# Two gate chunks beside the end of the attention, two more ahead of the first branch product, in a two-layer trunk on one Trainium2 core

## The chip, the cores and the metric

The kernel runs on one core of one Trainium2 chip. The metric is the device time of one execution, in microseconds; the median of three runs before the change is 2620.59 us (2617.87 to 2622.11). The profile comes from one further execution, which took 2614.91 us.

## What is computed

One inference step of a trunk of two layers over 128 context and 512 latent tokens (640 columns in all), width 1024, in fp32. Each layer normalizes and modulates its input, runs four token mixers on one input projection, merges them by gates, and adds a feed-forward part. Of the reference, what matters here:

```
def mixer(xn, lp, ctx, rope_cs):
    z = xn @ lp['w_in']
    ...
    y_attn = attention(q, k, v).reshape(b, l, MLA_HEADS * V_DIM)
    y_ssm, ssm_final = s5_branch(u_ssm, h0, ..., lp['w_glu'])
    y_fft = fourier_branch(u_fft)
    y_conv = g_b * short_conv(g_c * h_in, lp['conv_w'])
    branches = jnp.stack([y_ssm, y_fft, y_attn.astype(y_ssm.dtype), y_conv], axis=2)
    proj = jnp.einsum('blkw,kwd->blkd', branches, lp['w_branch'])
    gates = jax.nn.sigmoid(xn @ lp['w_gate'] + lp['b_gate']).reshape(b, l, N_BRANCH, D_MODEL)
    out = jnp.sum(gates * proj, axis=2) @ lp['w_out']
    return out, ckv_n, k_pe, ssm_final

def layer(x, cond, lp, ctx, rope_cs):
    sh_m, sc_m, g_m, sh_f, sc_f, g_f = modulation(cond, lp['w_ada'], lp['b_ada'])
    xn = rms_norm(x, lp['norm_mix_g']) * (1 + sc_m) + sh_m
    mix, ckv_n, k_pe, ssm_final = mixer(xn, lp, ctx, rope_cs)
    x = x + g_m * mix
```

## The kernel before

Tokens lie in the free dimension (two halves of 320 columns, one PSUM bank each), channels on the partitions. Each fp32 product is made of three matmuls of reduced type: high half times high half, low half of the weights, low half of the data. The halves are made on the way: a cast on ScalarE gives the high one (`whi`, `xh`, `yb`), a subtraction on VectorE the low one (`wlo`, `xl`, again `yb`, whose buffer first receives the raw tile).

`mixer_in` runs the attention (a generator whose steps are put between other work), four chunks of the short convolution, and then waits until the attention's generator is through. `mixer_out` then opens a pool and starts three things: the **merges**, the **SSM** (four blocks, `ssm_block`, as a side generator) and the **modulations** (a side generator).

- `merges` goes through 32 pairs of a gate and a branch product, in the order of branches 1, 3, 2, 0 with 8 output chunks d each. A gate is one chunk of 8 k steps of 6 matmuls (48 of 128x320), a sigmoid on ScalarE into a tile `m_s`. A branch product is 4 k steps (24 matmuls) on the tiles `yb` of the branch; VectorE multiplies it with the gate's tile into `acc` (L1434, or L1436 and L1437). Each gate stands one pair ahead of its product. The product's weights serve two values of d. The four `yb` tiles of the next branch are loaded by GpSimd's DMA queue (L1401), two before the last product of a branch and two behind it, and split (L320, L321). Chunks rotate through two PSUM tiles called `main`.
- An SSM block loads its factors, does two groups of 8 matmuls into `side` tiles, 16 copies to `s_t` on ScalarE (L1303 to L1306), multiplies and two scans on VectorE (L1315 to L1329), more multiplies, then 24 matmuls and an activation `s_y`. The decay tile `s_dec` has one buffer; GpSimd copies into it (L1280).
- `modulations` brings 32 pieces of 512 KB through one buffer (`ada`, L693), and VectorE makes two products with a running sum of each (L696), so that a load waits for the products of the piece before. Behind each eighth piece a bias is added (L698). The gate of the residual is among these sections.

The order on each engine is made ahead of the run by a scheduler from the order in which the program emits its work. Side generators are emitted by a planner's clock: it adds for each matmul about 0.136 us, and a generator comes on when the clock has passed its due time. The first modulation piece comes 12 us after the start, one each 10.5 us after that; the first SSM block 12 us after the start. By that clock a gate is about 6.5 us and a branch product about 3.3. What isn't done by the end of the merges is emitted there.

Behind the merges the output product runs (chunks of 48 matmuls on the `xh`, `xl` tiles, same two `main` tiles), and VectorE adds each chunk to the residual (`x`, L1457), which frees its banks for the chunk after next.

The lines that matter most: the gate ahead of its product, the SSM's start, and the constants

```
            if n + 1 < len(order):
                k2, d2 = order[n + 1]
                ...
                gate(k2, d2)
...
            def blocks():
                yield 12.0
...
MOD_START = (12.0, 90.0)
MOD_PACE = (10.5, 12.0)
```

Of the kernel before, what the change touches and what calls it, by code (L numbers as in the profile page):

```python
# [11 lines left out]
AF = mybir.ActivationFunctionType  # L12
# [7 lines left out]
KD = 8  # L20
LAT = 512
CTX = 128
NT = LAT + CTX
HALF = NT // 2
# [15 lines left out]
SSM_LOAD, SSM_STEP, SSM_LAST = 12.0, 3.0, 6.0  # L40
P_DELAY, PV_DELAY = 5.0, 1.8
TABLES_PACE = 1.5
ROT_START, ROT_PACE = 8.0, 6.0
MOD_START = (12.0, 90.0)
MOD_PACE = (10.5, 12.0)

V_GMIX, V_GFFN, V_BADA, V_BGATE, V_QA, V_KVA, V_GQ, V_GK, V_CONV, V_DSK, NV = (
    0, 8, 16, 64, 96, 99, 101, 102, 103, 115, 123)
# [157 lines left out]
class Program:  # L206
# [1175 lines left out]
        return out  # L1382


    def merges(self, pool, l, ycm, acc, xs, ssm):

        nc = self.nc
        two = lambda ap: ap.rearrange("p (a b) -> p a b", a=2)
        yb = lambda: self.t(pool, [128, NT], "yb", F32R, bufs=12)
        order = [(k, d) for k in (1, 3, 2, 0) for d in range(KD)]  # L1390
        ys = {k: [] for k in range(4)}
        sig, w, out = [], None, []

        def load(k, tiles):
            for i in tiles:
                hi, lo = yb(), yb()
                if k == 0:
                    self.split(hi, lo, ycm[i].rearrange("p t k -> p (t k)"))
                else:
                    y = lo.bitcast(F32)  # L1400
                    nc.gpsimd.dma_start(out=y, in_=self.d_br[l][{1: 1, 2: 0, 3: 2}[k]][i])  # L1401
                    self.split(hi, lo, y)
                ys[k].append((hi, lo))

        def gate(k, d):
            n = k * KD + d
            pg = self.chunk(self.A["wgate"][l, n], KD, xs)
            s = self.t(pool, [128, NT], "m_s")
            nc.scalar.activation(out=two(s), in_=pg[:, :, :HALF], func=AF.Sigmoid,
                                 bias=self.vec[l][:, V_BGATE + n:V_BGATE + n + 1])  # L1410
            sig.append(s)

        load(1, range(4))
        gate(*order[0])
        for n, (k, d) in enumerate(order):
            if k == 0 and d == 0:
                ys[0] = self.glu(pool, l, ycm, ys[0])
            if n + 1 < len(order):
                k2, d2 = order[n + 1]
                if d2 == 0:  # L1420
                    if k2 == 0:
                        self.need(ssm)
                    load(k2, range(2))
                gate(k2, d2)
            else:
                for i in range(KD - 1):
                    self.merged(l, acc, out, i)
            s = sig.pop(0)
            if d % 2 == 0:
                w = self.weights(self.A["wbr"][l, k, d // 2].rearrange("p a k m -> p (a k m)"), 1024)  # L1430
            pp = self.main_ps()
            self.gemm(pp, w, 512 * (d % 2), 128, 128, ys[k], range(4))
            if n < KD:
                self.anchor = nc.vector.tensor_mul(out=two(acc[d]), in0=pp[:, :, :HALF], in1=two(s))  # L1434
            else:
                self.anchor = nc.vector.tensor_mul(out=two(s), in0=pp[:, :, :HALF], in1=two(s))  # L1436
                nc.vector.tensor_add(out=acc[d], in0=acc[d], in1=s)  # L1437
            if d == KD - 1 and n + 1 < len(order):
                load(k2, range(2, 4))
        self.merged(l, acc, out, KD - 1)  # L1440
        return out

# [18 lines left out]
    def start(self, pool, x, norm, tags, tables):  # L1461
# [76 lines left out]
    def mixer_in(self, l, xs, first, tables):  # L1538

        nc, tc = self.nc, self.tc  # L1540
        A = self.A
        with tc.tile_pool(name=f"p1a{l}", bufs=8, reuse_waits="tile") as pa:
            with tc.tile_pool(name=f"p1f{l}", bufs=4, reuse_waits="tile") as pf:
                def consts(*names):
                    for name in names:
                        t = self.t(pa, {"cs": [128, 256], "ksel": [128, 64], "tk": [128, 6, 64], "selq": [128, 2, 32],
                                        "tq": [128, NT]}[name], name, bufs=1)
                        nc.sync.dma_start(out=t, in_=A[name])
                        setattr(self, name, t)
                if l > 0:  # L1550
                    self.tables = self.side(self.ssm_tables(tables, l, TABLES_PACE))
                lat = self.latents(pa, pf, l, xs, first, consts)
                for i in range(4):
                    self.ssm_input(pf, l, i, self.chunk(A["win"][l, 5 + i], KD, xs))
                consts("cs", "selq", "tq")
                dft = self.t(pf, [128, 2, 2, 257], "dft", bufs=1)
                nc.scalar.dma_start(out=dft, in_=A["dft"])
                dftc = self.t(pf, [128, 2, 128], "dftc", bufs=1)
                nc.scalar.dma_start(out=dftc, in_=A["dftc"])
                ff = []  # L1560
                for i in range(4):
                    ps = self.chunk(A["win"][l, 9 + i], KD, xs)
                    if i > 1:
                        self.need(ff[i - 2])
                    u = self.t(pf, [128, NT], "ct")
                    nc.scalar.copy(out=u.rearrange("p (a b) -> p a b", a=2), in_=ps[:, :, :HALF])
                    ff.append(self.side(self.fourier(pf, l, i, u, dft, dftc, ff[-1] if ff else None), True))
                self.need(*ff)
            with tc.tile_pool(name=f"p1k{l}", bufs=1, reuse_waits="tile") as pk:
                self.need(*lat)  # L1570
                self.keys_values(pk, pa, l)
                norms = self.queries(pk, pa, l)
                self.need(self.tables)
                tables.release()
                with tc.tile_pool(name=f"p1c{l}", bufs=3, reuse_waits="tile") as pc:
                    att = self.attention(pa, pc, l, norms)
                    self.rots = self.side(self.rotations(
                        l, lambda: self.t(pc, [128, 1024], "rotations", bufs=2), ROT_PACE, ROT_START))
                    for i in range(4):
                        self.conv(pc, l, i, xs)  # L1580
                    self.need(*att)
                    self.need(self.rots)

    def ssm_input(self, pool, l, i, ps):
        nc = self.nc
# [8 lines left out]
    def mixer_out(self, l, xs):  # L1594

        tc = self.tc
        with tc.tile_pool(name=f"p2{l}", bufs=2, reuse_waits="tile") as p:
            acc = [self.t(p, [128, NT], "acc", bufs=KD) for _ in range(KD)]
            ycm = [self.t(p, [128, 8, 80], "ycm", bufs=4) for _ in range(4)]

            def blocks():
                yield 12.0
                for b in range(4):
                    yield from self.ssm_block(p, l, b, ycm[b])
            ssm = self.side(blocks())
            self.modulations(p, l, range(2, 6), MOD_START[0], MOD_PACE[0], 1)
            ms = self.merges(p, l, ycm, acc, xs, ssm)
            self.need(self.modside)
            return ms

    def tail(self, l, ms):
# [107 lines left out]
    def emit(self):  # L1719
        with ExitStack() as ctx:  # L1720
            self.setup(ctx)
            ctx.enter_context(self.tc.manual_schedule(engines={mybir.EngineType.PE}))
            nc, tc = self.nc, self.tc
            tables = tc.alloc_tile_pool(name="p0t", bufs=2, side="right", reuse_waits="tile")
            with tc.tile_pool(name="p0", bufs=8, reuse_waits="tile") as p:
# [10 lines left out]
                xs, first = self.start(p, x, norm, tags, tables)  # L1736
            for l in range(L):
                if l == 0:
                    for k in range(KD):
                        self.tap(f"xh{l}_{k}", xs[k][0].bitcast(F32))  # L1740
                if l > 0:
                    tables = tc.alloc_tile_pool(name=f"p0t{l}", bufs=2, side="right", reuse_waits="tile")
                self.mixer_in(l, xs, first, tables)
                ms = self.mixer_out(l, xs)
                r = self.tail(l, ms)
                if r is not None:
                    xs, first = r
# [17 lines left out]
```

## Time and profile before

| what | value |
|---|---|
| median of 3 runs | 2620.59 us (2617.87 to 2622.11) |
| profiled execution | 2614.91 us, of which the span is 2613.1 |
| mean granted TensorE clock | 0.985 |
| instructions | 44975 |
| TensorE, VectorE, ScalarE, GpSimd busy | 97%, 69%, 40%, 7% of the span |
| HBM | 119 GB/s over the span |

The span is the time from the first to the last profiled instruction; 1.8 us of the execution lie around it. Layer 0 takes about the first half, layer 1 the second. In a timeline a row is a run of like instructions: start, duration, engine, line, operation, output and input tiles (buffer numbers left out), a count, and in brackets the idle time of the engine before it and what ended it. Neighbours on an engine overlap in part, so that the distance of two starts is shorter than a duration.

### The profile page before, as it was taken

What the parts mean: (1) busy time and instruction counts of PE and PEld (TensorE: products, weight loads), DVE (VectorE), ACT (ScalarE), POOL (GpSimd) and SP (SyncE); (2) the same over time, 40 slices, a digit from 0 to 9 for tenths busy, and PEclk for the clock granted to TensorE, in tenths of its full rate; (3) what the DMA queues carried; (4) which work ended last, traced back from release to release, by engine and by line L of the source; (5) the groups of instructions that cost most, each with busy time, mean ns of one, the idle gap of its engine ahead of it and who ended that gap; (6) DMA issues with size and microseconds to landing.
All of it is one profiled execution on the core that took longest, in us unless ns stands there. A gap on an engine that the chain in (4) does not pass through costs nothing.

```text
span 2613.1 us, 44975 instructions
## 1 busy us (share of the span) xinstructions
PE 2537.7 (97%) x18038; PEld 2434.7 (93%) x18038; DVE 1801.4 (69%) x3581; ACT 1054.0 (40%) x1793; POOL 188.6 (7%) x316
## 2 busy tenths in 40 slices
PE   7999999999999999999999999999999998999999
PEld 5988898999999899999979888989999998999999
DVE  5889764776555787876669897657676548666755
ACT  5335544333223543433453344443332226433433
POOL 0110000111000100000021100011200001000000
PEclk8999999999999999999999999999999999999999
DMA  6452115565444133433235322156644331222222
GB/s 254 130 157 96 54 61 175 166 210 172 129 122 155 51 104 119 122 97 88 79 115 151 123 98 74 46 185 207 197 158 125 118 113 57 82 82 89 79 79 86
DMA packets 121201, 313.85 MB, mean 120 GB/s; under 512 B 35616, under 2 KB 46432, under 8 KB 120608
## 3 DMA queue, kind: packets, MB, share of 16 engines
q1 hardware_dynamic: 101680, 250.52, 30.9%
q0 software_dynamic: 16432, 55.39, 6.2%
q10 hardware_dynamic: 2880, 5.06, 0.5%
q8 instruction: 142, 2.33, 0.4%
q14 instruction: 67, 0.55, 0.1%
HBM read 268.12 MB, written 42.80 MB: 119 GB/s over the span
## 4 chain that ended last, share of the span: by engine, by line
PE 82%; issue 10%; DVE 5%; ACT 3%; POOL 0%; DMA 0%; ACTq 0%; DVEq 0%; POOLq 0%
PE main L239 72%; PE side L239 8%; PE side L243 1%; DVE wlo L321 1%; DVE xl L543 1%; ACT xh L541 0%; ACT whi L320 0%; DVE tl L321 0%; ACT pq L1027 0%; DVE hh L569 0%; DMA yb<-d_br 0%; POOL d_r L1260 0%; DVE hh L538 0%; ACT P L924 0%; DVE hl L538 0%
## 5 line engine op out<-in xcount | busy, mean ns | idle before, releaser
L239 PE MATMUL main<-xh,whi 128*128 128x320 f32 x2848 | 740.0, 317 | 8.2 <-ACT xh L541 5.4
L239 PE MATMUL main<-xl,whi 128*128 128x320 f32 x2848 | 724.7, 312 | 6.7 <-DVE xl L321 4.5
L239 PE MATMUL main<-xh,wlo 128*128 128x320 f32 x2848 | 722.4, 311 | 0.0
L320 ACT CAST whi<-wraw 128x1024 fp32r<-128x1024 f32 (+2 forms) x318 | 297.6, 936 | 773.0 <-PE main L239 610.5
L239 PEld LDWEIGHTS main<-xh,whi 128*128 128x128 f32 x2848 | 494.7, 190 | 32.3 <-issue 19.3
L239 PEld LDWEIGHTS main<-xl,whi 128*128 128x128 f32 x2848 | 498.8, 190 | 11.5 <-DVE xl L321 5.7
L239 PEld LDWEIGHTS main<-xh,wlo 128*128 128x128 f32 x2848 | 499.2, 190 | 0.0
L321 DVE TENSOR_TENSOR wlo<-wraw,whi 128x1024 fp32r<-128x1024 f32 (+2 forms) x318 | 344.9, 1085 | 217.6 <-ACT whi L320 214.6
L239 PE MATMUL main<-yb,whi 128*128 128x320 f32 x1152 | 231.2, 312 | 4.4 <-ACT yb L320 4.4
L1457 DVE SCALAR_TENSOR_TENSOR x<-main,ada,x 128x320 f32<-128x320 f32 (+2 forms) x240 | 94.0, 434 | 193.2 <-PE main L239 193.0
L696 DVE SCALAR_TENSOR_TENSOR ada_j<-ada,ada_c 128x1024 bf16<-128x1024 f32 x160 | 194.8, 1217 | 3.8 <-DMA ada<-wada 3.2
L239 PEld LDWEIGHTS main<-yb,whi 128*128 128x128 f32 x1152 | 184.3, 189 | 5.3 <-ACT yb L320 4.9
L239 PE MATMUL main<-hh,whi 128*128 128x320 f32 x704 | 165.0, 310 | 1.0 <-ACT hh L320 1.0
L239 PE MATMUL main<-hl,whi 128*128 128x320 f32 x704 | 164.5, 309 | 0.0
L239 PE MATMUL main<-hh,wlo 128*128 128x320 f32 x704 | 164.3, 309 | 0.0
L239 PE MATMUL main<-th,whi 128*128 128x320 f32 x480 | 149.2, 311 | 0.0
L239 PE MATMUL main<-th,wlo 128*128 128x320 f32 x480 | 149.1, 311 | 0.0
L239 PE MATMUL main<-tl,whi 128*128 128x320 f32 x480 | 149.0, 310 | 0.0
L321 DVE TENSOR_TENSOR wlo<-wsum,whi 128x512 fp32r<-128x512 f32 (+1 forms) x120 | 103.6, 864 | 51.9 <-ACT whi L320 50.6
L320 ACT CAST whi<-wsum 128x512 fp32r<-128x512 f32 (+1 forms) x120 | 91.6, 763 | 114.9 <-PE main L239 110.5
L239 PE MATMUL main<-yb,wlo 128*128 128x320 f32 x576 | 132.0, 311 | 0.0
L239 PEld LDWEIGHTS main<-hh,whi 128*128 128x128 f32 x704 | 118.6, 188 | 4.1 <-issue 2.6
(346 smaller groups left out, 3766.6 us busy)
## 6 DMA issues: line engine op xcount, KB each, us to landing
ada<-wada SPq DMA_DIRECT2D x96, 512.0 KB, 4.2
wraw<-wfi SPq DMA_DIRECT2D x88, 512.0 KB, 3.5
wraw<-wgate SPq DMA_DIRECT2D x64, 512.0 KB, 3.6
wraw<-win SPq DMA_DIRECT2D x50, 512.0 KB, 3.6
wraw<-wfo SPq DMA_DIRECT2D x48, 384.0 KB, 3.2
wraw<-wbr SPq DMA_DIRECT2D x32, 512.0 KB, 3.6
d_f<-t_G POOLq DMA_DIRECT2D x16, 512.0 KB, 4.7
d_et<-t_et POOLq DMA_DIRECT2D x16, 512.0 KB, 4.6
```

Of the source, the lines that this page charges most:

```text
L239: self.nc.tensor.matmul(out, lhsT, rhs, **kw)
L243: self.nc.tensor.transpose(out, in_, ident)
L320: self.nc.scalar.copy(out=hi, in_=src)
L321: self.nc.vector.tensor_sub(out=lo, in0=src, in1=hi.bitcast(F32))
L543: nc.vector.scalar_tensor_tensor(out=xl[:, a:b], in0=t[:, a:b], scalar=B[:, s:s + 1], in1=xh.bitcast(F32)[:, a:b], op0=ALU.add, op1=ALU.su ...
L696: nc.vector.scalar_tensor_tensor(out=junk, in0=w, scalar=1.0, in1=sc[:, s, :], op0=ALU.mult, op1=ALU.mult, accum_out=self.ada[l][:, o + t, ...
L1457: self.anchor = nc.vector.scalar_tensor_tensor(out=x[:, o:o + n], in0=p, scalar=gcol[:, s:s + 1], in1=x[:, o:o + n], op0=ALU.mult, op1=ALU ...
```

## The change

The list of pairs goes to module level. A method `gate` makes one gate chunk and its sigmoid. `mixer_in` emits the first two gates behind the convolution chunks and ahead of the point where the attention has to be through, with the sigmoids in tiles of the convolution's pool, which stays open and is handed on. `merges` begins with these two, emits two more gates ahead of the first branch product, and then none until the third; from there each gate stands one pair ahead, as before. Behind the second product the convolution's pool is closed, a pool for the SSM's tiles is opened, and the SSM is started, without the 12 us of delay. The first two tiles of the next branch are loaded ahead of the gate instead of behind it. The modulations' start and pace are the same.

```diff
+MERGES = [(k, d) for k in (1, 3, 2, 0) for d in range(KD)]
...
+    def gate(self, l, n, xs, s):
+        pg = self.chunk(self.A["wgate"][l, n], KD, xs)
+        self.nc.scalar.activation(out=s.rearrange("p (a b) -> p a b", a=2), in_=pg[:, :, :HALF], func=AF.Sigmoid,
+                                  bias=self.vec[l][:, V_BGATE + n:V_BGATE + n + 1])
+        return s
...
         load(1, range(4))
-        gate(*order[0])
+        done = len(sig)
         for n, (k, d) in enumerate(order):
             if k == 0 and d == 0:
                 ys[0] = self.glu(pool, l, ycm, ys[0])
-            if n + 1 < len(order):
-                k2, d2 = order[n + 1]
-                if d2 == 0:
-                    if k2 == 0:
-                        self.need(ssm)
-                    load(k2, range(2))
-                gate(k2, d2)
-            else:
+            if d == KD - 1 and n + 1 < len(order):
+                if order[n + 1][0] == 0:
+                    self.need(ssm)
+                load(order[n + 1][0], range(2))
+
+            while done < min(n + 2 if n else 4, len(order)):
+                kg, dg = order[done]
+                sig.append(self.gate(l, kg * KD + dg, xs, self.t(pool, [128, NT], "m_s")))
+                done += 1
+            if n + 1 == len(order):
...
+            if n == 1:
+                ssm = start_ssm()
...
+                sig = [self.gate(l, MERGES[n][0] * KD + MERGES[n][1], xs, self.t(pc, [128, NT], "ct"))
+                       for n in range(2)]
+                self.need(*att)
+                self.need(self.rots)
+        return pc, sig
...
+            pc, sig = early
+            pools = []
+
             def blocks():
-                yield 12.0
                 for b in range(4):
-                    yield from self.ssm_block(p, l, b, ycm[b])
-            ssm = self.side(blocks())
+                    yield from self.ssm_block(pools[0], l, b, ycm[b])
+
+            def start_ssm():
+                pc.release()
+                pools.append(tc.alloc_tile_pool(name=f"p2s{l}", bufs=2, side="right", reuse_waits="tile"))
+                return self.side(blocks())
```

How this moves instructions, at three places. Lines of the changed file are one higher from the list on.

TensorE at the end of the attention in layer 0, before: scores (`side<-ak,at`), transposes of softmax rows (`side<-ident,P`), products with v (`side<-PT,v`), and the first gate (`main<-xh,whi`).

```order
L239 MATMUL side_728_4642<-ak_4288,at_4236 128x128
L243 MATMUL side_731_4653<-ident,P_4625 128x128
L243 MATMUL side_733_4657<-ident,P_4649 128x128
L239 MATMUL side_733_4657<-PT_4655,v_2140 64x128
L239 MATMUL side_733_4657<-PT_4659,v_2140 64x128
L239 MATMUL main_4713<-xh_185,whi_4709 128x320 x2
```

The same place in the change, from the last product with v of the block before.

```order
L240 MATMUL side_723_4604<-PT_4610,v_2140 64x128
L240 MATMUL main_4649<-xh_185,whi_4645 128x320 x2
L240 MATMUL main_4649<-xh_185,wlo_4646 128x320 x2
L240 MATMUL main_4649<-xl_186,whi_4645 128x320 x2
L244 MATMUL side_733_4656<-ident,P_4625 128x128
L240 MATMUL side_735_4660<-ak_4288,at_4235 128x128
L240 MATMUL side_735_4660<-ak_4289,at_4235 128x128
L240 MATMUL side_735_4660<-ak_4288,at_4236 128x128
L240 MATMUL main_4649<-xh_187,whi_4645 128x320 x2
```

The first gate's chunk has moved ahead of the two last transposes: one of its 8 k steps stands ahead of the first, four between the two, three behind the second.

VectorE at the end of the merges in layer 0, before, from the last branch product's multiply (`m_s<-main`) to the first residual (`x<-main_1225`); `ada_j` rows are the modulation products of one piece.

```order
L1436 TENSOR_TENSOR m_s_8298<-main_8365,m_s_8298 128x640
L696 SCALAR_TENSOR_TENSOR ada_j_4686,ada_89<-ada_8327,ada_c_4683 128x1024
L321 TENSOR_TENSOR wlo_8556<-wraw_8553,whi_8555 128x1024
L1437 TENSOR_TENSOR acc_4678<-acc_4678,m_s_8298 128x640
L696 SCALAR_TENSOR_TENSOR ada_j_4686,ada_89<-ada_8327,ada_c_4683 128x1024
L321 TENSOR_TENSOR xl_8393<-acc_4678,xh_8392 128x640
L698 TENSOR_TENSOR ada_89<-ada_89,vec_72 128x16
L1457 SCALAR_TENSOR_TENSOR x_8414<-main_1225_8436,ada_89,x_8414 128x320
```

The same place in the change, from the last sum of the merges on.

```order
L1438 TENSOR_TENSOR acc_4791<-acc_4791,m_s_8238 128x640
L697 SCALAR_TENSOR_TENSOR ada_j_4799,ada_89<-ada_8278,ada_c_4796 128x1024
L322 TENSOR_TENSOR xl_8388<-acc_4791,xh_8387 128x640
L697 SCALAR_TENSOR_TENSOR ada_j_4799,ada_89<-ada_8393,ada_c_4796 128x1024
L322 TENSOR_TENSOR wlo_8621<-wraw_8618,whi_8620 128x1024
L697 SCALAR_TENSOR_TENSOR ada_j_4799,ada_89<-ada_8393,ada_c_4796 128x1024
L697 SCALAR_TENSOR_TENSOR ada_j_4799,ada_89<-ada_8397,ada_c_4796 128x1024
L322 TENSOR_TENSOR wlo_8682<-wraw_8679,whi_8681 128x1024
L697 SCALAR_TENSOR_TENSOR ada_j_4799,ada_89<-ada_8397,ada_c_4796 128x1024
L699 TENSOR_TENSOR ada_89<-ada_89,vec_72 128x16
L1460 SCALAR_TENSOR_TENSOR x_8418<-main_1225_8440,ada_89,x_8418 128x320
```

Two more pieces, with four products, and two weight splits now stand between the last branch product and the first residual.

VectorE around the split of the third and fourth tile of the second branch (`yb<-yb,yb`), before: the end of SSM block 1 and the sum of branch product 7 (`acc<-main_5699`); the block's scans stand twelve rows ahead of the first of these rows.

```order
L1337 TENSOR_TENSOR s_t_5677<-s_R_5353,s_t_5559 128x648
L1339 TENSOR_TENSOR s_X_5678<-s_t_5676,s_t_5677 64x640
L1340 TENSOR_TENSOR s_X_5678<-s_t_5676,s_t_5677 64x8x64
L696 SCALAR_TENSOR_TENSOR ada_j_4686,ada_89<-ada_5565,ada_c_4683 128x1024
L321 TENSOR_TENSOR wlo_5805<-wraw_5802,whi_5804 128x1024
L696 SCALAR_TENSOR_TENSOR ada_j_4686,ada_89<-ada_5565,ada_c_4683 128x1024
L1341 TENSOR_TENSOR s_X_5678<-s_t_5676,s_t_5677 64x8x16
L1342 TENSOR_TENSOR s_fin_5600<-s_t_5676,s_t_5677 128x8
L1434 TENSOR_TENSOR acc_4678<-main_5699,m_s_5579 128x640
L321 TENSOR_TENSOR yb_5730<-yb_5730,yb_5729 128x640
L321 TENSOR_TENSOR wlo_5897<-wraw_5894,whi_5896 128x1024
L321 TENSOR_TENSOR yb_5735<-yb_5735,yb_5734 128x640
```

In the change, from the scans of SSM block 1 (`s_t<-s_dec,s_t`) on; the sum of branch product 7 stands seven rows ahead of them.

```order
L1330 SCALAR_TENSOR_TENSOR s_t_5765<-s_dec_5536,s_t_5688 128x648
L1330 SCALAR_TENSOR_TENSOR s_t_5767<-s_dec_5536,s_t_5739 128x648
L1337 TENSOR_TENSOR s_t_5802<-s_R_5534,s_t_5765 128x648
L322 TENSOR_TENSOR wlo_5920<-wraw_5917,whi_5919 128x1024
L1338 TENSOR_TENSOR s_t_5803<-s_R_5534,s_t_5767 128x648
L697 SCALAR_TENSOR_TENSOR ada_j_4799,ada_89<-ada_5551,ada_c_4796 128x1024
L1340 TENSOR_TENSOR s_X_5804<-s_t_5802,s_t_5803 64x640
L697 SCALAR_TENSOR_TENSOR ada_j_4799,ada_89<-ada_5551,ada_c_4796 128x1024
L322 TENSOR_TENSOR yb_5700<-yb_5700,yb_5699 128x640
L1341 TENSOR_TENSOR s_X_5804<-s_t_5802,s_t_5803 64x8x64
L322 TENSOR_TENSOR yb_5705<-yb_5705,yb_5704 128x640
```

The splits stood behind all of block 1's work and another product's sum; now block 1 is two products later, and they stand among its work, behind the scans.

## Rows read from the trace of the kernel before

**Rows 1.** The page, part 1: engine, busy us (share), instructions.
```profile
PE 2537.7 (97%) x18038; PEld 2434.7 (93%) x18038; DVE 1801.4 (69%) x3581; ACT 1054.0 (40%) x1793; POOL 188.6 (7%) x316
```

**Rows 2.** TensorE's timeline, attention end, layer 0: start, us, ..., [idle before <-releaser].
```profile
410.67 0.71 PE L239 MATMUL side<-ak,at 128*128 128x128 f32 x3 [1.58 <-ACT P L924]
...
411.28 0.45 PE L243 MATMUL side<-ident,P 128*128 128x128 f32 x1
...
413.20 0.45 PE L243 MATMUL side<-ident,P 128*128 128x128 f32 x1 [1.47 <-DVE P L927]
...
414.62 0.90 PE L239 MATMUL main<-xh,whi 128*128 128x320 f32 x2
...
423.16 0.46 PE L239 MATMUL main<-xh,whi 128*128 128x320 f32 x2
```

**Rows 3.** The same in layer 1.
```profile
1703.26 0.55 PE L239 MATMUL side<-ak,at 128*128 128x128 f32 x3 [1.58 <-ACT P L924]
...
1707.08 0.90 PE L239 MATMUL main<-xh,whi 128*128 128x320 f32 x2
...
1716.15 0.46 PE L239 MATMUL main<-xh,whi 128*128 128x320 f32 x2
```

**Rows 4.** TensorE's timeline, first branch product and next gate, both layers.
```profile
430.20 0.46 PE L239 MATMUL main<-yb,whi 128*128 128x320 f32 x2
...
434.39 0.58 PE L239 MATMUL main<-yb,whi 128*128 128x320 f32 x2 [2.26 <-ACT yb L320]
...
437.55 0.73 PE L239 MATMUL main<-xh,whi 128*128 128x320 f32 x2
...
1723.19 0.46 PE L239 MATMUL main<-yb,whi 128*128 128x320 f32 x2
...
1730.07 0.73 PE L239 MATMUL main<-xh,whi 128*128 128x320 f32 x2
```

**Rows 5.** Two lone waits; windows behind them: us, TensorE busy (x), PEclk, DMA share, GB/s.
```profile
297.10 1.15 PE L239 MATMUL side<-ak,at 128*128 128x320 f32 x6 [1.28 <-ACT P L924]
...
297.00:304.00 7.00, 6.90 (x57) 1.00 0.16 62
...
1434.73 2.38 PE L239 MATMUL side<-cs,ct 128*128 128x128 f32 x10 [1.69 <-DVE ct L1013]
...
1435.00:1441.80 6.80, 5.80 (x23) 0.51 0.58 170
```

**Rows 6.** Layer 0's tail: ScalarE's and TensorE's timeline at the normalization.
```profile
859.49 1.28 ACT L487 ACT_TABLE_LOAD   x1
...
863.45 0.35 PE L239 MATMUL side<-hl,ones 128*128 128x128 f32 x1 [0.95 <-DVE hl L491]
```

**Rows 7.** End of the merges, layer 0: VectorE, then TensorE's third output chunk.
```profile
811.96 1.22 DVE L696 SCALAR_TENSOR_TENSOR ada_j<-ada,ada_c 128x1024 bf16<-128x1024 f32 x1
...
813.10 0.08 DVE L696 DVE_READ_ACCUMULATOR ada_j<-ada,ada_c 128x1 f32 x1
...
815.10 1.14 DVE L1457 SCALAR_TENSOR_TENSOR x<-main,ada,x 128x320 f32<-128x320 f32 x3 [1.09 <-PE main L239]
...
822.08 0.46 PE L239 MATMUL main<-xh,whi 128*128 128x320 f32 x2
```

**Rows 8.** Modulation pieces, all loads: issue to landing.
```profile
DMA to landing us min/median/max: 3.3/4.2/9.9
```

**Rows 9.** SSM block 1, layer 0: TensorE, VectorE, GpSimd.
```profile
497.82 2.35 PE L239 MATMUL side<-s_u,s_EF 128*128 128x80 f32 x20
...
505.80 0.82 DVE L1316 TENSOR_TENSOR s_t<-s_R,s_t 128x648 f32<-128x648 f32 x1
...
509.76 2.90 DVE L1329 TENSOR_TENSOR_SCAN s_t<-s_dec,s_t 128x648 f32<-128x648 f32 x2
...
512.78 1.19 POOL L1280 COPY s_dec<-s_mg 128x648 f32<-128x648 f32 x1 [15.56 <-issue]
```

**Rows 10.** Branch tiles, all loads: issue to landing.
```profile
DMA to landing us min/median/max: 3.1/4.6/6.8
```

More of the change, by code (lines that the diff above doesn't have):

```diff
@@ L1382, in glu, with merges @@
         return out
-    def merges(self, pool, l, ycm, acc, xs, ssm):
+    def gate(self, l, n, xs, s):
[3 more added lines that the diff above has]
+        return s
+    def merges(self, pool, l, ycm, acc, xs, sig, start_ssm):
         nc = self.nc
@@ L1389, in merges @@
         yb = lambda: self.t(pool, [128, NT], "yb", F32R, bufs=12)
-        order = [(k, d) for k in (1, 3, 2, 0) for d in range(KD)]
+        order = MERGES
         ys = {k: [] for k in range(4)}
-        sig, w, out = [], None, []
+        w, out = None, []
         def load(k, tiles):
@@ L1403, in load @@
                 ys[k].append((hi, lo))
[L1405 to L1411, printed above, removed]
         load(1, range(4))
-        gate(*order[0])
+        done = len(sig)
         for n, (k, d) in enumerate(order):
@@ L1438, in merges @@
             if d == KD - 1 and n + 1 < len(order):
-                load(k2, range(2, 4))
+                load(order[n + 1][0], range(2, 4))
+            if n == 1:
+                ssm = start_ssm()
         self.merged(l, acc, out, KD - 1)
@@ L1574, in mixer_in @@
                 tables.release()
[L1575 to L1582, printed above, removed]
+                pc = tc.alloc_tile_pool(name=f"p1c{l}", bufs=3, side="right", reuse_waits="tile")
+                att = self.attention(pa, pc, l, norms)
+                self.rots = self.side(self.rotations(
+                    l, lambda: self.t(pc, [128, 1024], "rotations", bufs=2), ROT_PACE, ROT_START))
+                for i in range(4):
+                    self.conv(pc, l, i, xs)
+                sig = [self.gate(l, MERGES[n][0] * KD + MERGES[n][1], xs, self.t(pc, [128, NT], "ct"))
[3 more added lines that the diff above has]
+        return pc, sig
     def ssm_input(self, pool, l, i, ps):
@@ L1592, in ssm_input, with mixer_out @@
             nc.sync.dma_start(out=self.d_u[l][8 * i + g].rearrange("s c k -> c s k"), in_=u[16 * g:16 * g + 16])
-    def mixer_out(self, l, xs):
+    def mixer_out(self, l, xs, early):
         tc = self.tc
@@ L1599, in mixer_out @@
             ycm = [self.t(p, [128, 8, 80], "ycm", bufs=4) for _ in range(4)]
+            pc, sig = early
+            pools = []
             def blocks():
-                yield 12.0
                 for b in range(4):
-                    yield from self.ssm_block(p, l, b, ycm[b])
-            ssm = self.side(blocks())
+                    yield from self.ssm_block(pools[0], l, b, ycm[b])
[3 more added lines that the diff above has]
+                return self.side(blocks())
             self.modulations(p, l, range(2, 6), MOD_START[0], MOD_PACE[0], 1)
-            ms = self.merges(p, l, ycm, acc, xs, ssm)
+            ms = self.merges(p, l, ycm, acc, xs, sig, start_ssm)
             self.need(self.modside)
+            pools[0].release()
             return ms
@@ L1742, in emit @@
                     tables = tc.alloc_tile_pool(name=f"p0t{l}", bufs=2, side="right", reuse_waits="tile")
-                self.mixer_in(l, xs, first, tables)
-                ms = self.mixer_out(l, xs)
+                early = self.mixer_in(l, xs, first, tables)
+                ms = self.mixer_out(l, xs, early)
                 r = self.tail(l, ms)
```

## Prediction

> **What bounds the kernel now.** I read the shares first: TensorE is busy for 2537.7 us, 97% of the span [rows 1], so only what makes TensorE wait, or slows its clock, counts; VectorE's or GpSimd's work counts where TensorE waits for it. Then TensorE's timeline, for idle time ahead of an instruction, at the places that the change touches. At the end of the attention of layer 0 it waits 1.58 and 1.47 us for the last softmax rows [rows 2]; the first of these stands in layer 1 as well [rows 3]. In the first branch product it waits 2.26 us for the cast of a branch tile [rows 4]. After each of these places the matmuls are slow for a while: in 1435.00 to 1441.80, behind a wait of 1.69 us, the granted clock is 0.51, near the low one of the two levels (1.2 against 2.4 GHz); behind a lone 1.28 us it stays at 1.00 [rows 5]. Otherwise the merges run without a wait of size. Third, the SSM blocks on VectorE and the last modulation pieces, since the change moves both against the branch products.
>
> **What is gained.** (a) Attention end. In layer 0 the last large PV product ends at 409.09 (410.67 less the wait) and the second gate chunk starts at 423.16, 14.07 us later, of which 7.04 is gate 0 at full clock (48 matmuls, 0.88 us for each of 8 k). In the new order gate 0 lies between the transposes: one k ahead of the first, four ahead of the second, three behind it. The first softmax block is ready for its transpose at 411.28 [rows 2], k 0 ends at 409.97, so 1.3 us of wait stay; the second wait (1.47) has 3.5 us of matmuls over it. With 1.1 us for the transposes, scores and PV, gate 1 starts 9.45 us after the PV product: gain 4.6. In layer 1 gate 1 starts at 1716.15, 14.5 us after the PV product's end (1703.26 less 1.58; gate 0, from 1707.08, needs 9.07 instead of 7.04 [rows 3]): gain 5.0. A lone wait of 1.28 us cost no clock and 1.69 us did [rows 5]; I take none for 1.3 and keep 1.7 per layer as the other end. Sum 9.6.
>
> (b) First branch product. It starts at 430.20 and the next gate at 437.55; 24 matmuls need 3.52, so 3.83 us go, and 0.3 more in the gate's first k: 4.1. In layer 1 it is 1723.19 to 1730.07, 3.36, and 0.7 in the gate [rows 4]: 4.1. With gates 2 and 3 ahead of it, branch 0 starts near 439.6 and the tile that it waited for until 434.39 is there. Gain 8.2, nothing takes its place.
>
> (c) The next layer's conditioning vector is loaded and put through its activation inside the merges instead of beside the tail; the activation-table load of 1.28 us ahead of the normalization's rstd, and with it TensorE's 0.95 us [rows 6], should go: 1.0, in layer 0 alone. Sum of the gains 18.8.
>
> **What is paid.** (d) End of the merges. The modulation pieces follow a clock of the planner: the first 12 us after the merges' code starts, then one each 10.5, 32 of them, to 348 us. Two gates now lie ahead of that start, so the merges' planned length shrinks from about 349 to 336 us and the last **two** pieces come behind the last branch product. VectorE's order shows it: four more scalar products and two more weight splits stand ahead of the first residual than before. All pieces share one buffer, so each load waits for the products before it. With the times of before: the last old product ends at 813.18 [rows 7]; load issued, landed 4.2 us later (3.3 to 9.9 [rows 8]) at 817.4; product, split, product at 1.22 each, 821.0; load, 825.2; three more, 828.8; sum, three residuals (1.14), 830.0. The third chunk of the output product needs the banks that the first residual frees; it starts at 822.08 [rows 7]. Wait 7.7 us (6.0 with landings of 3.3, 9.5 with 5), in both layers: the orders are alike.
>
> For one transfer the Trainium skill (DMA: Bandwidth & Descriptors, Anatomy of one DMA) fits about 2.0 us plus the bytes over 436 GB/s; for 512 KB that is an estimate of 3.2 us, and the wait would be about 5.7 us. The rows say 4.2, which decides.
>
> (e) Branch product 8, first of the second branch. SSM block 1 stood in branch product 5 and stands now in product 7, because the SSM begins later. Take its start on TensorE as S, with the times of before (S is 497.82 [rows 9]). TensorE: 3.5 us for the block, 0.9 for the rest of product 7, 7.0 for gate 9, two k: it needs the low half of the third tile at S+13.8. VectorE: behind the block's copies on ScalarE the second multiply starts at S+8.0, the scans end at S+14.8 [rows 9], and in the new order the split of the third tile stands **behind** them: a multiply 0.75, a weight split 1.2 to 1.7, a multiply 0.75, two modulation products of 1.15 (1.22 less the overlap of neighbours), a subtraction 0.8, then the split itself, 0.8. That is S+21.9. The fourth tile's load waits on GpSimd behind the decay copy (512.78, 1.19 us), which waits for the scans: issued near S+16.5, landed 4.6 us later (3.1 to 6.8 [rows 10]), cast, split at S+23.3. TensorE waits 8.1 and then 0.4: 8.5 us (5.5 if the products and splits are quicker, 11 at the longest landing). Before, two gates, two products and the next block's output lay between block 1 and product 8.
>
> (f) Branch product 16. Block 3 has moved in the same way, into product 15. With its own start as S, TensorE needs the low half at S+15.3; the split stands behind the scans (S+15.2, a weight cast being 0.4 later there), one weight split and one multiply: S+17.9, a wait of 2.6; the next tile is at S+21.3 when TensorE is at S+18.8: 2.5. Sum 5.1 (2.5 to 8).
>
> (g) Clock. Behind each of (d) to (f) I take what followed waits of 1.5 to 2.3 us [rows 2 to 4]: gate 0 at 8.54 and 9.07 instead of 7.04, and 4.1 - 2.26 = 1.8 behind branch 0's wait: 1.5 to 2.0, and I take 1.9 each. The ends are 0 (a lone 1.28) and 3.4 (half of 6.8 us in [rows 5]). Six places: 11.4.
>
> Edits at nothing: the SSM buffers' own pool, the gate method, the list on module level; they move no busy engine beyond what is counted. Loads of block 0's factors start only after product 1, so the block may come a little late; I put that with the rivals. SP's later loads queue behind the two late pieces, but their weights are needed over 20 us later.
>
> **The sum.** Losses per layer 7.7 + 8.5 + 5.1 = 21.3, twice 42.6, clock 11.4: 54.0. Gains 18.8. Net +35.2 on the profiled execution's 2614.9 us: 2650. That execution lies 5.7 us under the median of 2620.6, so I forecast **2656**, 1.3% slower.
>
> **Rivals.** Covers hold (faster): VectorE brings the splits by S+13.8 and S+15.3 and the pieces by 822, so only the gains remain: 2620.6 - 18.8 = 2602. For it: the same engines fed these products without a wait before. Against: the order on VectorE is fixed, and the scans alone end later than S+13.8. It decides from a chain about 8 us shorter than that of [rows 9].
> One place of three (no change): if only the merges' end bites, 2 x 9.6 = 19.2 meets the gains: 2621. For it: its two loads in a row rest on the fewest assumptions. Against: (e) has the same kind of fixed order.
> Clock and more waits (slower still): each wait costs 3.4 instead of 1.9 (+9), the attention's remaining wait costs clock as well (+3.4), block 0's factors come 2 us late in each layer (+4): 2672. For it: the waits of (d) and (e) are three times as long as those that the 1.9 comes from. The Trainium skill (TensorE: Matmul & The Clock Gate, What's actually happening) says that the low clock is the default and activity lifts it; by that rule this rival would hold. The rows agree that waits come ahead of the low clock, but one of 1.28 us did not bring it [rows 5].
> That the change doesn't do what it says (gate 0 doesn't hide the transposes) would take 9.6 from the gains: 2665, inside the range.
>
> **How the numbers follow.** Forecast 0.68, more waits 0.15, one place 0.07, covers 0.10. The range: lowest losses 6.0 + 5.5 + 2.5 twice and no clock, 28 - 18.8 = +9, 2630; highest 9.5 + 11 + 8 twice, clock 20.4, less gains of 15.4: +62, 2682. The two rivals below, 0.17, stay out. A measurement here can tell about 0.2% (5.2 us) from no change. Faster 0.10, same 0.07, slower 0.83.
>
> **What would show it.** Gate 1 of layer 0 starting 9.5 us after the last PV product, full clock in branch 0; a wait of TensorE for VectorE's branch split of 7 to 9 us in product 8 and about 5 in product 16, in both layers; one for VectorE's residual of 7 to 8 us in the third chunk of the output product, with two modulation loads issued behind the last branch product. I am wrong if product 8 starts its third tile without a wait, or if the last two pieces' loads are issued before the last branch product ends.

## The result and the profile after

The changed kernel takes 2657.22 us (median of 4 executions, 2651.27 to 2664.49) where the kernel before takes 2620.14 (4 executions, 2617.87 to 2622.11). The ratio is 1.0158, with a 95% interval of 1.0131 to 1.0185. That is slower, near the 2656 forecast and inside its range. The profiled execution took 2657.94 us, its span is 2656.2 and its mean granted clock 0.981 (0.985 before). On a second chip the unaltered changed kernel came out at 1.0151 (1.0123 to 1.0180).

TensorE does the same 18038 matmuls in nearly the same busy time as in [rows 1]. The page of after, part 1 (engine, busy us, share, instructions):

```profile
PE 2544.8 (96%) x18038; PEld 2440.8 (92%) x18038; DVE 1805.0 (68%) x3581; ACT 1054.9 (40%) x1793; POOL 186.4 (7%) x316
```

The matmuls are the same, so I read the 7.1 us more of busy time (2544.8 less 2537.7) as a lower clock (0.981 against 0.985); the rest of the difference is waiting. TensorE's waits of after (engine, tile, line waited for; us in total, times, longest), first in 385 to 900 us (layer 0), then in 1700 to 2200 us (layer 1):

```profile
PE main L240 <- DVE x L1460: 9.9, 1, 9.9
PE main L240 <- DVE yb L322: 9.8, 3, 5.8
PE main L240 <- ACT yb L321: 1.7, 2, 0.9
PE side L240 <- DMA s_EF<-d_et: 1.5, 1, 1.5
...
PE main L240 <- DVE yb L322: 9.3, 3, 6.2
PE main L240 <- DVE x L1460: 7.7, 1, 7.7
PE side L240 <- DMA s_EF<-d_et: 3.0, 1, 3.0
```

In both layers the two large items are those forecast: the branch tiles' splits (`yb`, steps e and f) and the first residual (`x`, step d). The third, `s_EF`, the factors of SSM block 3, is not in the prediction at that place.

**The attention's end**, layer 0, TensorE's timeline of after, which answers to [rows 2]:

```profile
403.54 1.31 PE L240 MATMUL side<-PT,v 128*64 128x128 f32 x20
...
407.04 0.30 PE L244 MATMUL side<-ident,P 128*128 128x128 f32 x1 [1.11 <-DVE P L928]
...
414.24 0.56 PE L240 MATMUL main<-xh,whi 128*128 128x320 f32 x2
```

The products with v end at 404.85 and gate 1 starts at 414.24, 9.4 us later (14.07 before). The second wait is gone and the first is 1.11 us.

**Branch product 8**, layer 0: VectorE from the scans of SSM block 1 to the split that TensorE waits for, then TensorE.

```profile
517.97 2.90 DVE L1330 TENSOR_TENSOR_SCAN s_t<-s_dec,s_t 128x648 f32<-128x648 f32 x2
...
521.52 1.75 DVE L322 TENSOR_TENSOR wlo<-wraw,whi 128x1024 fp32r<-128x1024 f32 x1
523.18 0.82 DVE L1338 TENSOR_TENSOR s_t<-s_R,s_t 128x648 f32<-128x648 f32 x1
523.93 1.21 DVE L697 SCALAR_TENSOR_TENSOR ada_j<-ada,ada_c 128x1024 bf16<-128x1024 f32 x1
...
525.81 1.21 DVE L697 SCALAR_TENSOR_TENSOR ada_j<-ada,ada_c 128x1024 bf16<-128x1024 f32 x1
526.95 0.81 DVE L322 TENSOR_TENSOR yb<-yb,yb 128x640 fp32r<-128x640 f32 x1
...
527.82 1.44 PE L240 MATMUL main<-yb,whi 128*128 128x320 f32 x4 [5.84 <-DVE yb L322]
```

VectorE is never idle here, and what keeps the split back is what the order put ahead of it.

**The end of the merges**, layer 0, which answers to [rows 7]: SP's two loads of the late pieces, VectorE's product behind each with its idle time, the first residual, and TensorE's third output chunk.

```profile
819.42 0.33 SPq L694 DMA_DIRECT2D ada<-wada  x1
...
829.33 0.33 SPq L694 DMA_DIRECT2D ada<-wada  x1
...
825.79 1.23 DVE L697 SCALAR_TENSOR_TENSOR ada_j<-ada,ada_c 128x1024 bf16<-128x1024 f32 x1 [5.65 <-DMA ada<-wada]
...
834.16 1.23 DVE L697 SCALAR_TENSOR_TENSOR ada_j<-ada,ada_c 128x1024 bf16<-128x1024 f32 x1 [4.86 <-DMA ada<-wada]
...
837.80 2.17 DVE L1460 SCALAR_TENSOR_TENSOR x<-main,ada,x 128x320 f32<-128x320 f32 x6
...
838.39 1.28 PE L240 MATMUL main<-xh,whi 128*128 128x320 f32 x2 [9.94 <-DVE x L1460]
```

**The clock behind the waits.** Windows of 9 us of after (us; busy time and instructions of TensorE, its weight loads, VectorE, ScalarE, GpSimd; granted clock; DMA share; GB/s): behind the attention's wait, product 8, block 3's factors, product 16 and the residual of layer 0, then the factors of layer 1. Behind product 8, product 16 and the residual of layer 1 the clock is 0.70, 0.84 and 0.66.

```profile
407.00:416.00 9.00, 8.96 (x63) 8.62 (x64) 2.13 (x6) 3.09 (x6) 0.54 (x1) 1.00 0.30 97
527.80:536.80 9.00, 8.98 (x45) 8.98 (x46) 8.90 (x16) 1.45 (x2) 0.95 (x4) 0.71 0.55 164
618.70:627.70 9.00, 9.00 (x69) 9.00 (x70) 3.50 (x5) 5.73 (x18) 2.96 (x6) 1.00 0.80 188
640.80:649.80 9.00, 9.00 (x47) 9.00 (x48) 8.87 (x16) 0.00 (x0) 0.39 (x1) 0.73 0.21 58
838.40:847.40 9.00, 8.96 (x44) 8.64 (x45) 1.57 (x5) 1.74 (x3) 0.00 (x0) 0.71 0.11 46
1934.80:1943.80 9.00, 8.95 (x47) 8.98 (x48) 0.83 (x1) 3.69 (x15) 1.13 (x2) 0.62 0.71 141
```

What a place loses is 9 us times what the clock lacks to 1.00: 2.4 to 3.4 us at six of the nine places, the factors of layer 1 among them, 1.4 us behind product 16 of layer 1, and nothing behind the attention's wait and the factors of layer 0.

**Where the time went, by stage.** The table gives the stretch of TensorE's timeline from the attention's first product with v (`side<-PT,v`) to the first sum of squares behind the merges' output product (`side<-hh,ones`). The stretch holds every place that the prediction speaks of but the normalization of step (c). It starts at 259.16 us in before and 254.96 in after; that difference lies ahead of anything the change touches. The last column is TensorE's busy time in the two stretches together; what is left of their length is waiting.

| kernel | layer 0, us | layer 1, us | TensorE busy, both, us |
|---|---|---|---|
| before | 579.7 | 579.8 | 1142.7 |
| after | 602.9 | 606.0 | 1155.2 |
| after, second chip | 603.3 | 607.7 | 1159.0 |
| modulation pace alone (`mod_pace`) | 590.7 | 591.1 | 1148.1 |
| SSM delay alone (`ssm_late`) | 589.4 | 589.4 | 1149.1 |
| both edits (`both`) | 581.5 | 578.9 | 1143.4 |
| both, longer lead of the factors (`both_load16`) | 574.2 | 571.6 | 1135.1 |

After loses 23.2 and 26.2 us here, 49.4 in all, while its profiled execution is only 43.0 longer. The start (253 to 259 us over all kernels) and the stretch between the layers (709 to 716 us) vary by a few us from execution to execution; in this one they came out 6.4 us shorter than in that of before.

### The profile page after: what moved, and what is told of

Its sections match the earlier page's. It is cut to its first block, busy times and chain, and to the rows that moved or that the text cites. A ratio compares the mean times of both kernels' runs of the same rounds, so it can differ in the third digit from the quotient of the medians.

```text
span 2656.2 us, 44949 instructions
## 1 busy us (share of the span) xinstructions
PE 2544.8 (96%) x18038; PEld 2440.8 (92%) x18038; DVE 1805.0 (68%) x3581; ACT 1054.9 (40%) x1793; POOL 186.4 (7%) x316
## 4 chain that ended last, share of the span: by engine, by line
PE 81%; DVE 8%; issue 6%; ACT 3%; DMA 2%; POOL 0%; ACTq 0%; DVEq 0%; POOLq 0%
PE main L240 70%; PE side L240 9%; PE side L244 2%; DVE wlo L322 1%; DMA s_EF<-d_et 1%; DMA ada<-wada 1%; DVE xl L544 1%; DVE sm L922 1%; DVE ada_j L697 0%; ACT xh L542 0%; ACT whi L321 0%; DVE tl L322 0%; ACT P L925 0%; ACT pq L1028 0%; DVE P L928 0%
## 5 line engine op out<-in xcount | busy, mean ns | idle before, releaser
L240 PE MATMUL main<-yb,whi 128*128 128x320 f32 x1152 | 233.9, 315 | 23.6 <-DVE yb L322 19.2
```

The costliest lines, as they stand in the source:

```text
L240: self.nc.tensor.matmul(out, lhsT, rhs, **kw)
```

## The experiments

**The late modulation pieces (step d).** `mod_pace` changes the planner's pace:

```
-MOD_PACE = (10.5, 12.0)
+MOD_PACE = (9.8, 12.0)
```

> The changed kernel with one number altered: the first pace of the modulation pieces is 9.8 us instead of 10.5 us of the planner's clock. By the order on VectorE no modulation product then stands between the last sum of the merges and the first residual. Theory (two late pieces make the third output chunk wait): the waits of 9.94 us (layer 0) and 7.72 us (layer 1) go, and the slow clock behind them (2.6 and 3.1 us, from 6.8 us at a granted clock of 0.62 and 0.55): 23 us less, 2634 us, with the waits in branch products 8 and 16 still there (6 to 8 and 4 to 5 us). Rival (something else, such as the output weights, holds that chunk as well): the wait gets another releaser and at least half stays, 2645 us or more.

Measured: 2637.81 us, ratio to before 1.0081 (1.0051 to 1.0111), some 20 us less than after (1.0158 less 1.0081, of 2614). The wait for the residual is gone in both layers, nothing takes its place there, and the waits in products 8 and 16 stay. The wait for block 3's factors falls too, from 1.5 and 3.0 us to under 0.5 and to 0.7, so the gain is not the residual's alone.

So the late pieces were the cause of the wait for the residual. `one_piece` takes away only one of them, by an earlier start and a pace of 10.0:

```
-MOD_START = (12.0, 90.0)
-MOD_PACE = (10.5, 12.0)
+MOD_START = (4.0, 90.0)
+MOD_PACE = (10.0, 12.0)
```

> The changed kernel with the modulation pieces started at 4 instead of 12 us and paced 10.0 instead of 10.5 us: by VectorE's order one piece less is late, four modulation products stand ahead of the first residual in place of six (two in the kernel before, none with a pace of 9.8). Theory (each late piece costs a load and two products in a row): the wait in the third output chunk falls from 7.7 to 9.9 us by one load and two products, 6 to 8 us, to 2 to 3 us in both layers; 2642 to 2646 us. Rival (the wait has one cause however many pieces are late): it stays at 7 us or more, 2655 us.

Measured: 2640.06 us, ratio 1.0087 (1.0065 to 1.0110), as with none late. The wait isn't 2 to 3 us but gone. SP's load of the one late piece, VectorE's first product on it and the first residual, layer 0:

```profile
823.57 0.33 SPq L694 DMA_DIRECT2D ada<-wada  x1
...
827.70 1.23 DVE L697 SCALAR_TENSOR_TENSOR ada_j<-ada,ada_c 128x1024 bf16<-128x1024 f32 x1 [3.43 <-DMA ada<-wada]
...
831.35 1.69 DVE L1460 SCALAR_TENSOR_TENSOR x<-main,ada,x 128x320 f32<-128x320 f32 x4
```

From load to residual it takes 7.8 us (831.35 less 823.57). In [rows 7] the last old product ends at 813.18 and the third chunk starts at 822.08, so 8.9 us are covered: one piece fits under it with about a microsecond to spare, and the second costs all that it takes. My expectation of 2 to 3 us was a slip: the prediction's chain, one load and two products shorter (7.7 less 4.2 less 3.6), ends at zero.

**The SSM blocks against the tile splits (steps e, f).** `ssm_late` puts 10 us of the planner's clock ahead of the first block:

```
             def blocks():
+                yield 10.0
                 for b in range(4):
```

> The changed kernel with a delay of 10 us of the planner's clock ahead of the first SSM block. Blocks 1 and 3 then stand behind branch products 8's and 16's tile splits on VectorE: the splits come ahead of the scans. Theory (the splits behind the scans make TensorE wait): the waits in product 8 (6.7 and 8.0 us) and 16 (4.8 and 4.0) go, with their slow clock (about 2.5 each, 10 in all): 33 us less, 2624 us; if the wait for the SSM factors in block 3 (1.5 and 3.0 us, some 3.4 us of clock) goes too, 2616. The waits for the residual stay at 8 to 10 us. Rival (the splits are late for another reason, the tiles' loads or VectorE's load in general): waits for a branch tile of 4 us or more stay in product 8, 2645 us or more.

Measured: 2628.06 us, ratio 1.0051 (1.0031 to 1.0070), some 28 us less than after. No wait for a branch tile is left in either layer; the rival falls. What stays in layer 0:

```profile
PE main L240 <- DVE x L1460: 8.0, 1, 8.0
PE side L240 <- DMA s_EF<-d_et: 3.7, 2, 3.0
```

The wait for the SSM factors didn't go; it is 3.7 and 2.3 us.

**Both edits.** `both` has the two edits above.

> The changed kernel with both edits: modulation pace 9.8 us instead of 10.5, and the 10 us of delay ahead of the first SSM block. Theory: the costs of the two add up and nothing else is lost, so 23 and 33 to 41 us go: 2593 to 2601 us, faster than the kernel before by the gains that were forecast (18.8 us, 2602). Rival (the earlier pieces fill VectorE and SP's queue in the second half of the merges, and a new wait comes up): 2610 us or more.

Measured: 2609.59 us, ratio 0.9980 (0.9960 to 1.0000): the 2593 to 2601 of the theory are missed, and the rival's new wait is there. The stretch of the table is back at the length of before, no shorter. With both forecast losses gone, the gains of (a) and (b) are eaten by waits for SSM factors (`s_EF`, `s_M`), in layer 0 as shown and 4.1 us of the same in layer 1:

```profile
PE side L240 <- DMA s_EF<-d_et: 3.3, 2, 3.1
...
PE side L240 <- DMA s_M<-d_k: 1.6, 1, 1.6
```

The block's loads stand on SP's queue a fixed 12 us of the planner's clock ahead of its matmuls, behind whatever SP still has to issue. SP ahead of block 3 in layer 0 of `both`, and TensorE's start of the block:

```profile
601.42 7.40 SPq L694 DMA_DIRECT2D ada<-wada  x2
...
615.99 0.33 SPq L694 DMA_DIRECT2D ada<-wada  x1
...
616.91 0.52 SPq L1272 DMA_DIRECT2D s_EF<-d_et  x1
...
626.75 6.71 PE L240 MATMUL side<-s_u,s_EF 128*128 128x80 f32 x32 [3.13 <-DMA s_EF<-d_et]
```

The factors' load is issued right behind a modulation load at 615.99, and 9.8 us pass from its issue to the first matmul, 3.1 of them waiting: TensorE came 6.7 us behind the issue. In the kernel before it came 9.5 us behind it in both layers and did not wait. A late issue and a slow transfer look alike to TensorE, and a longer lead covers either; which of the two it was, no run separates. `both_load16` gives a longer lead:

```
-SSM_LOAD, SSM_STEP, SSM_LAST = 12.0, 3.0, 6.0
+SSM_LOAD, SSM_STEP, SSM_LAST = 16.0, 3.0, 6.0
...
-                yield 10.0
+                yield 6.0
```

> The two edits together as before (modulation pace 9.8 us, SSM delayed), with the time between an SSM block's loads and its first matmuls raised from 12 to 16 us of the planner's clock, and the delay ahead of the first block 6 us instead of 10, so that the first block stays in its place. Theory (in the kernel with both edits the gain is eaten by waits for the SSM factors, 1.6 and 3.1 us in layer 0, 0.8, 1.3 and 2.0 in layer 1, with some 8 us of slow clock behind them, since the loads stand too close ahead of the block in SP's queue): the waits fall under 0.6 us and 10 to 17 us go, 2595 to 2600 us where the kernel before takes 2614. Rival (the loads are late because the transfers are slow, or VectorE is the next limit): waits of over 1 us stay and the time is within 4 us of 2610.

Measured: 2597.60 us (2594.71 to 2603.05), ratio 0.9929 (0.9910 to 0.9948) with the kernel before at 2618.67. The factors' waits are gone in both layers. The largest left in layer 0:

```profile
PE main L240 <- DVE m_s L1437: 2.3, 3, 0.9
```

This version is the fastest of all here. It is faster than before by 18.6 us (0.0071 of 2618.67; 13.6 to 23.6 by the interval), where the prediction's gains alone were 18.8. In the stretch of the table it gains 5.5 and 8.2 us, 13.7 in all, so that the agreement with 18.8 is in part luck.

**The gains apart.** `gates_behind` emits the first two gates behind the attention's end instead of ahead of it and leaves the rest of the changed kernel as it is:

```
-                sig = [self.gate(l, MERGES[n][0] * KD + MERGES[n][1], xs, self.t(pc, [128, NT], "ct"))
-                       for n in range(2)]
                 self.need(*att)
                 self.need(self.rots)
+                sig = [self.gate(l, MERGES[n][0] * KD + MERGES[n][1], xs, self.t(pc, [128, NT], "ct"))
+                       for n in range(2)]
```

> The changed kernel with one move undone: the first two gates are emitted behind the end of the attention instead of ahead of it; everything behind stays, so branch product 0 has its four gates ahead of it. Theory (gate 0 hides the waits for the last softmax rows): 4.6 and 5.0 us come back, and up to 3.4 us of clock: 2667 us (2665 to 2670), with waits of 1.5 us twice at the attention's end in layer 0. Rival (gate 0 between the transposes hides nothing that costs): within 2 us of the changed kernel, 2657 us.

Measured: 2668.76 us, ratio 1.0199 (1.0172 to 1.0227), 0.41% or 11 us over the changed kernel by the ratios. The two waits of before are back:

```profile
407.78 0.55 PE L240 MATMUL side<-ak,at 128*128 128x128 f32 x3 [1.58 <-ACT P L925]
...
410.16 0.30 PE L244 MATMUL side<-ident,P 128*128 128x128 f32 x1 [1.48 <-DVE P L928]
```

From the attention's first product with v to branch product 0 this kernel takes 184.7 and 184.5 us, the changed one 180.5 and 180.2: (a) is worth 4.2 and 4.3.

`both_two_gates` is `both` without the two extra gates ahead of branch product 0; the SSM's delay is made longer to keep its blocks in place:

```
-            while done < min(n + 2 if n else 4, len(order)):
+            while done < min(n + 2, len(order)):
...
-                yield 10.0
+                yield 16.5
```

> The kernel with both edits, with one more move undone: no two extra gates ahead of branch product 0 (each gate stands one pair ahead of its product, as in the kernel before), and the SSM's delay 16.5 us instead of 10, which puts its blocks at the same places among the branch products. Theory: TensorE waits 1.5 to 2.5 us in branch product 0 for a cast of a branch tile, with slow clock behind it, 4.1 us in each layer: 8 us more than the kernel with both edits, 2618 us. Rival (the extra gates gain nothing, since the two gates ahead suffice): within 3 us of 2610.

Measured: 2638.18 us, ratio 1.0080 (1.0062 to 1.0099), 26 us over `both` instead of 8. TensorE waits twice in branch product 0, and ScalarE's order tells why (layer 0):

```profile
424.16 0.90 PE L240 MATMUL main<-yb,whi 128*128 128x320 f32 x2 [2.57 <-ACT yb L321]
429.64 0.91 PE L240 MATMUL main<-yb,whi 128*128 128x320 f32 x2 [3.51 <-ACT yb L321]
...
423.38 0.72 ACT L321 CAST yb<-yb 128x640 fp32r<-128x640 f32 x1 [6.20 <-DMA yb<-d_br]
...
425.77 1.28 ACT L685 ACT_TABLE_LOAD   x1
427.06 1.91 ACT L685 ACTIVATE ada_c<-ada_c 128x2048 f32<-128x2048 f32 x1
428.88 3.22 ACT L321 CAST yb<-yb 128x640 fp32r<-128x640 f32 x5
```

The first wait is for the first cast, at 423.38 (423.23 in after); the second is for the next cast, which stands behind a table load and the conditioning vector's activation. TensorE arrives earlier, since gate 0 has gone beside the attention: product 0 starts 169.2 us behind the attention's first product with v, 171.0 in before. And the first tile comes later: its cast is 168.4 us behind that product, 163.9 in before. Gate 0 has put off the attention's last product with v (159.0 us, 154.8 in before), and on GpSimd's queue the store of the attention's output stands ahead of the first tile's load. First the store in before, then store and load here:

```profile
415.40 0.54 POOL L998 DMA_DIRECT2D d_br<-at  x1 [6.14 <-DVE at L994]
...
415.06 0.54 POOL L999 DMA_DIRECT2D d_br<-at  x1 [10.00 <-DVE at L995]
416.85 0.56 POOL L1408 DMA_DIRECT2D yb<-d_br  x1 [1.24 <-issue]
```

The store is 156.2 us behind the first product with v in before and 160.1 here. So TensorE waits 6.1 us instead of the 2.26 of [rows 4]. From the first product with v to the first matmuls of SSM block 0, with the same gates and products ahead of it in both, `both` takes 213.1 and 212.9 us, this kernel 222.5 and 221.9. So the two extra gates are worth 9.4 and 9.0 us once the first two are moved. The remaining 7 to 8 us of the 26 were not forecast; in layer 0 block 1 waits 5.31 us for `s_M` where it waits 1.59 in `both`.

**The changed kernel on a second chip**, unaltered:

> The changed kernel once more, unaltered, beside the runs below, so that they are compared on one chip. The kernel before took 2614.4 us in the runs of the four first experiments and 2620.1 beside the changed one; both theories expect the same difference as then, 35 to 43 us over the kernel before.

Measured: 2659.14 us, ratio 1.0151 (1.0123 to 1.0180), 39.5 us over the kernel before. Its third output chunks wait 7.23 and 6.83 us, its product 8 waits 6.7 and 7.1, and block 3's factors 2.11 and 4.07.

## Why the prediction was right, and where its sum was off

The sign and the place of each forecast loss held, and the two edits that remove them leave the gains. That the point came out within 2 us is luck: in the touched stretch 49.4 us were lost where the steps, without the 1.0 us of (c) that lies outside it, give 36.2.

- **(a) attention's end**: forecast 4.6 and 5.0, measured 4.2 and 4.3. Gate 1 came 9.4 us behind the products with v (9.45 said), the wait that stays is 1.11 (1.3 said) and cost no clock, as taken.
- **(b) first branch product**: 8.2 forecast. No wait is left there. With (a) it makes 8.4 us in each layer: going from the kernel before to `gates_behind`, product 0 starts 13.7 and 13.4 us later for two gates of 7.04, so 0.4 and 0.7 are gained ahead of it, and the 3.83 and 3.36 of [rows 4] in it. The sum held, but treating (a) and (b) as independent was wrong. By `both_two_gates` (b) is worth 9 us once (a) is there, and (a) without (b) is worth nothing: that kernel has (a) alone up to the gate behind product 0, with the same work as before, and reaches this gate 179.4 and 178.8 us behind the attention's first product with v, where before takes 178.4 and 178.0. The prediction took the tile as unmoved; (a) makes it come later.
- **(c)** the table load ahead of rstd is gone from layer 0's tail, and TensorE has no wait there. Its 1.0 us can't be told from the variation of the stretch between the layers.
- **(d) merges' end**: 7.7 per layer forecast, 9.94 and 7.72 measured (7.23 and 6.83 on the second chip). The mechanism was right to the row; layer 0's excess is the two landings, after which VectorE had been idle 5.65 and 4.86 us, where 4.2 were taken for a whole landing. The Trainium skill (DMA: Bandwidth & Descriptors, Anatomy of one DMA) would make a landing 3.2 us, an estimate by its fit, and the wait 5.7; but that section gives the fit for transfers that GpSimd issues, and these loads are SP's. The trace has longer landings, and the median of [rows 8] was the better guide.
- **(e) product 8**: 8.5 forecast; 6.7 in layer 0 (0.86 and 5.84) and 8.0 in layer 1 (0.86, 6.18 and 0.95). The 0.86 is a wait for ScalarE's cast of a tile, which the chain did not have.
- **(f) product 16**: 5.1 forecast; 4.8 in layer 0 (0.86, 1.78 and 2.20) and 4.0 in layer 1. In (e) and (f) the order of the splits and scans was right, and the terms are 1 us too large on average.
- **(g) clock**: this term was mis-sized. I took 1.9 us at each of six places, 11.4. The six places' waits make 41.2 us and block 3's factors 4.5. With the gains of 16.8 (twice 8.4), 49.4 plus 16.8 is 66.2, which leaves 20.5 us of slow clock. Of these 3.4 lie behind the factors of layer 1 and 17.1 at the six places, 2.8 to 2.9 each on average. The windows behind the six show 1.4 to 3.1, 14.9 in all; where the other 2 us lie stays open. The busy times of the table say the same without the gains: after is busy 20.1 us longer than `both_load16`, whose granted clock is 1.00 in both stretches. The upper end of 3.4 was also misread: the 1.69 us of [rows 5] is not a lone wait, another of 0.99 us follows at 1438.10, inside its window.
- **Not in the sum**: the factors of SSM block 3, 1.54 and 2.96 us with 3.4 of clock in layer 1, 7.9 us. The prediction spoke of late factors only as a part of a rival, and there of block 0, whose loads had been moved. It did not look at SP's queue ahead of the other blocks, though each had moved against the modulation loads. Block 3's factors took 10.0 and 11.4 us to land here, where none took over 9.0 in before, and TensorE came 8.6 us behind their issue in both layers instead of 9.5; the run does not say which weighs more.

Of the rivals, the one that the covers hold and the one in which one place bites fell by the waits above. That with clock and more waits (2672) was right in its parts: the clock at 2.8 to 2.9 per place lies between 1.9 and 3.4, and factors did come late, in block 3. Waits and clock were 3.1 us (45.7 less 42.6) and 9.1 us (20.5 less 11.4) over the sum, and the gains 1.0 under it: 13.2 us in all, 49.4 less 36.2. Between the medians 37 us are left of the 49.4 (41 by the ratio): the profiled execution of after was 6.4 us quicker outside the touched stretch, and that of before lies 5.7 us under its median.

## What to carry over

When work is moved ahead of a stage whose side work is timed by a planner, work out again how much of the side work comes too late: one late piece hid under the chunks that followed it, a second cost all that it took. What feeds a stage that now starts sooner must come sooner too, or a cover must be put ahead of it, as the two extra gates were. And read the order on every queue at the new places: the scans ahead of the splits on VectorE brought waits of 23.5 us in products 8 and 16 (6.7, 8.0, 4.8 and 4.0), and the SSM's factors, which stand behind other loads on SP's queue, came late without being forecast.

## What the runs showed of the hardware

The clock is not set by the length of a wait alone. Windows of 9 us behind waits for SSM factors, in order `both` behind 1.59 us, `gates_behind` behind 2.58 us, `both_two_gates` behind 1.58 us, `both` behind 3.13 us:

```profile
522.30:531.30 9.00, 8.96 (x69) 9.00 (x70) 3.91 (x6) 3.80 (x16) 1.47 (x3) 1.00 0.82 267
...
1944.80:1953.80 9.00, 8.97 (x69) 9.00 (x70) 3.28 (x4) 4.96 (x17) 1.14 (x2) 1.00 0.73 169
...
640.30:649.30 9.00, 8.97 (x47) 9.00 (x48) 2.44 (x4) 3.80 (x16) 0.00 (x0) 0.62 0.84 214
...
626.80:635.80 9.00, 9.00 (x42) 9.00 (x43) 1.55 (x2) 3.80 (x16) 0.00 (x0) 0.52 0.72 180
```

A lone wait of 2.58 us cost nothing and one of 1.58 us cost 3.4. Between 1.5 and 2.6 us the same kind of wait cost either; waits of up to 1.3 us that stood alone cost nothing in the merges, and behind each one from 2.9 us on the windows show a loss of 1.9 us or more. The Trainium skill (TensorE: Matmul & The Clock Gate, What's actually happening) says that the moment of the switch isn't aligned with the kernel and differs from run to run; the same place of the changed kernel, block 3 of layer 0, lost nothing behind 1.54 us in one execution and 3.4 us behind 2.11 in another, on the second chip, which agrees with that but doesn't prove it. A flat price for each wait, as in step (g), is therefore a mean at best.
